# DeltaNet values: from TensorE transposes to VectorE block transposes and a round trip through DRAM

## The chip, the cores and the metric

The kernel runs on one core of one Trainium2 chip. Time is the device time of one execution in microseconds (us), and the median of three executions is given. TensorE (PE in the profile, PEld for its weight loads), VectorE (DVE), ScalarE (ACT), GpSimd (POOL) and SyncE (SP, which issues nearly all DMAs) each work through a queue of their own in order. SBUF is the working memory, PSUM takes the results of TensorE, and what is called a DRAM tensor here is scratch in the chip's main memory.

## The reference

One layer of a hybrid decoder block on a sequence of 1024 tokens with a model width of 2048, all float32:

```
h = rmsnorm(x, ln_g);  proj = h @ w_in
(g_u, g_v, g_z, d_q, d_k, d_v, d_z, d_a, d_b, c_q, c_z) = split(proj)
out_a = gmlp_spatial_gating(g_u, g_v, ...) * silu(g_z)
q, k, v = split(causal_conv_silu(concat([d_q, d_k, d_v]), conv_w))   # 4 taps, 8 heads x 128
o = gated_delta_rule(l2norm(q) * 128**-0.5, l2norm(k), v, g, beta)
out_b = rmsnorm(o, dn_norm_g) * silu(d_z)
out_c = cross_attention(c_q, mem) * silu(c_z)
y = rmsnorm(x + concat([out_a, out_b, out_c]) @ w_out, final_g)
```

In the delta rule of a chunk the values enter as `vb = v * beta`, with one row for each token. The convolution, however, runs along the sequence, so the kernel computes it with channels on the partitions and tokens along the free dimension. Between the two stands a transpose of each head's values, 128 channels x 512 tokens in each half of the sequence.

## The kernel before

**The main stream.** The two large products (`h @ w_in`, `mixed @ w_out`) are done as seven half-size products instead of eight (`seven`, with sums and differences of the halves of both factors). Each of them is a `triple` in a rounded format: the high part times the high part, high times low and low times high. A piece of two weight blocks arrives by DMA in `raw` or `kept`, ACT rounds it to `rhi`, DVE subtracts to get `rlo`; a piece of the left factor goes through `lh` and `ll` (or `lm`) in the same way. There are two buffers of `rhi` and `rlo`. A piece feeds 36 products of 128x512 where a stage has six PSUM banks (`acc` 107 to 110, `dn` 113 and 114), 24 where it has four.

**What runs beside it.** The DeltaNet of eight heads in two halves of the sequence (`hf` 0 and 1) is done in pairs of heads. `front` makes queries and keys and stores them (`late_d`); `inverse` solves 32x32 triangles for four pairs at once in 31 steps on DVE; `levels` joins them to 128x128 blocks on PE; `values` makes the values; `scan_step` runs the recurrence over four tiles of 128 tokens; `heads_out` normalizes the result. `back_of` calls `front_late`, `levels`, `values` and `back` for a pair. Pairs 0 and 1 of both halves run beside the stage of the columns `zv`, pairs 2 and 3 in later stages.

**Values.** For each head `conv` loads 512 tokens (and three before) of the projected values from the DRAM tensor `pd` into `xr`, one of three buffers of 128x515; ACT multiplies the last tap into a tile `tn`, DVE adds the three others, and ACT applies Silu in `tn`. Then `to_tokens` has PE transpose the four 128x128 blocks against `ident` into a PSUM bank that the scan uses too (`dn_111` in the rows below), and `by_token` has ACT copy each block with the token's scale `hs` into the `vs` tile of the pair. Eight pair-halves of two heads make 16 such units and 64 transposes.

**A round trip that is there already.** `turn(tile, src, dst)` transposes on DVE within 32x32 blocks and stores the tile to DRAM; `turned_in(o, src)` loads it back in four DMAs that each put one group of 32 partitions in its place, so that the blocks change places and the whole is transposed. `heads_out` uses it for the scan's output, by the DRAM tensors `od`.

**What sets the order.** Nothing is issued as it is written: `Plan` records every instruction with a cost of its own, computes the dependencies by overlapping regions, lays the work out with a list scheduler in several passes, keeps the best and issues it. A change to one step therefore rebuilds the order of all engines. All instructions carry the line of the issuing loop, L398, so rows are told apart by tile names.

Of the kernel before, what the change touches and what calls it, by code (L numbers as in the profile page):

```python
# [11 lines left out]
AF = mybir.ActivationFunctionType  # L12
# [5 lines left out]
P = 128  # L18
# [4 lines left out]
HT = 512  # L23
# [3 lines left out]
NG, NH, NX = 4, 8, 4  # L27
# [374 lines left out]
def kernel(  # L402
# [29 lines left out]
    V, S, G, PE, Q = R.dve, R.act, R.pool, R.pe, R.sp  # L432
    rank, behind = R.rank, R.behind

    def C(shape, name, dt=F32):
        return sb.tile(list(shape), dt, name=name, tag=name)[:]

    def DT(shape, name, dt=F32):
        return dr.tile(list(shape), dt, name=name, tag=name)[:]
# [41 lines left out]
    def tok(ap):  # L481

        return ap.rearrange("p (t c) -> p t c", c=P)
# [22 lines left out]
    jk = C([P, HT], "jk", mybir.dt.bfloat16)  # L506
# [4 lines left out]
    turn = {"acc": 0, "tp": 0, "dn": 0}  # L511
# [224 lines left out]
    for mt in range(2):  # L736
        t = [ring["ai"](F32R) for _ in range(2)]
# [9 lines left out]
    for h in range(NX):  # L747
        t = ring["vs"](F32R).rearrange("p (s m) -> p s m", s=2)
# [60 lines left out]
    def over(bufs):  # L809
        r = Ring("", 0, None)  # L810
        r.bufs = bufs
        return r
# [38 lines left out]
    r3, ww = ([steps[:, i * P : (i + 1) * P] for i in two] for two in ((0, 1), (2, 3)))  # L851
    scs = [C([P, 12, NT, NH], f"sc{hf}") for hf in range(2)]
    gcs, ecs = ([DT([NT, NH, P], f"{n}{hf}") for hf in range(2)] for n in ("gcd", "ecd"))
    e_d = [[DT([P, NT, P], f"ed{hf}_{h}") for h in range(NH)] for hf in range(2)]
    scan_banks, work = dnr.bufs[0:2], over(dnr.bufs[0:2])
    dnab = over(scan_banks)
# [68 lines left out]
    def to_tokens(*pairs):  # L925
        with R.together():
            for src, tp in pairs:
                for tt in range(NT):
                    PE.transpose(tp[:, tt * P : (tt + 1) * P], src[:, tt * P : (tt + 1) * P], ident)
        return [tok(tp) for src, tp in pairs]  # L930

    def four(t, order):

        return t.rearrange(f"p ({order}) -> p t b i", b=4, t=NT)

    def turn(tile, src, dst):

        V.transpose(four(tile, "b t i"), four(src, "t b i"))
        Q.dma_start(dst, tile)

    def turned_in(o, src):

        v = src.rearrange("(a j) (b n) -> b j a n", a=4, b=4)
        for b in range(4):
            Q.dma_start(o[b * 32 : (b + 1) * 32].rearrange("j (a n) -> j a n", a=4), v[b])

    def conv(which, h, hf, o):
        ct = which * NH + h
        xr = ring["xr"]()
        w = [cw[:, k * 24 + ct : k * 24 + ct + 1] for k in range(4)]  # L950
        if hf == 0:
            G.memset(xr[:, 0:3], 0.0)
            Q.dma_start(xr[:, 3:], p_d[which][h][:, 0:HT])
        else:
            Q.dma_start(xr, p_d[which][h][:, HT - 3 :])
        S.activation(o, xr[:, 3:], AF.Copy, scale=w[3])
        for k in range(3):
            V.scalar_tensor_tensor(o, xr[:, k : k + HT], w[k], o, op0=ALU.mult, op1=ALU.add)
        S.activation(o, o, AF.Silu)

    def by_token(o, src, scale):
        for tt in range(NT):
            S.activation(o[:, tt], src[:, tt], AF.Copy, scale=scale[:, tt : tt + 1])

    def sumsq(o, src):
        for tt in range(NT):
            S.activation(jk[:, 0:P], src[:, tt], AF.Square, accum_out=o[:, tt : tt + 1])

    def qk(h, hf, tiles, hs, gt, bank):

# [2 lines left out]
        beta, edk = (scs[hf][:, i] for i in (0, 4))  # L973
        (kt,) = to_tokens((k, bank))
        sumsq(hs[:, 1], kt)
        V.tensor_scalar(hs[:, 1], hs[:, 1], EPS, None, op0=ALU.add)
        V.reciprocal(hs[:, 3], hs[:, 1])
# [204 lines left out]
    def front(p, hf, banks):  # L1182

        hp = (2 * p, 2 * p + 1)
        gt = ring["gt"]().rearrange("p (h t i) -> p h t i", h=2, i=P)
        for i, h in enumerate(hp):
            tiles, hs = front_sets(), ring["hs"]()
            conv(1, h, hf, tiles[1])
            conv(0, h, hf, tiles[0])
            qk(h, hf, tiles, hs, gt[:, i], banks[i])  # L1190
            V.tensor_copy(late_hs[:, hf, h], hs[:, 0:5:4])
            for d, t in zip(late_d[hf][h], tiles[:4]):
                Q.dma_start(d, t)
        gdr = blocks_out(gt, f"{hf}{p}")
        Q.dma_start(gt_d[hf][p].rearrange("p (h t i) -> p h t i", h=2, i=P), gt)
        return gdr
# [17 lines left out]
    def values(hf, hp, gt, qs, ks, hss, rest, inv):  # L1214
        for i, h in enumerate(hp):
            v = ring["tn"]()
            conv(2, h, hf, v)
            bank = scan_banks[i]
            by_token(rest[i][2], to_tokens((v, bank))[0], hss[i][:, 4])

    def back(hf, hp, gt, qs, ks, hss, rest, inv, ut=None):
        ut = ut or levels(gt, *inv)
# [339 lines left out]
    scan_banks, work = [dnr.bufs[0]] * 2, over(dnr.bufs[0:1])  # L1562
    gdrs = []

    def back_of(p, hf, inv):
        state = front_late(p, hf, inv)
        ut = levels(state[2], *state[-1])
        values(*state)
        back(*state, ut)
# [106 lines left out]
    scan_banks, work = dnr.bufs[0:2], over(dnr.bufs[2:3])  # L1676
# [46 lines left out]
    for n, (tag, to) in enumerate((("gt", mkT), ("inv", mv))):  # L1723
        for i in range(NX // 2):
            t = ring[tag](F32R).rearrange("p (h s m) -> p h s m", h=2, s=2)
# [196 lines left out]
```

## Time and profile before

| what | value |
| --- | --- |
| median of three executions | 1594.31 us (1592.87 to 1595.48) |
| the profiled execution | 1593.81 us, span 1592.1 us |
| granted TensorE clock, mean | 0.997 |
| busy: PE, DVE, ACT, POOL | 1570.2, 1228.7, 963.3, 106.7 us |
| instructions in the span | 24568 |
| moved by DMA | 434.12 MB, 273 GB/s mean |
| value transposes on PE | 64, from 617.1 to 1168.4 us |

The span runs from the first to the last instruction; the device time has 1.7 us more around it. Busy time of PE is the union of overlapping matmuls, so the price of one is read from the distance of starts, not from its duration. In a row of groups the columns are: engine, operation, out<-in, shape and count, then busy us and mean ns of one, then the idle time ahead and what ended it. A number in square brackets in the timeline is idle time just before the row, with its releaser.

### The profile page before, as it was taken

What the parts mean: (1) busy time and instruction counts of PE and PEld (TensorE: products, weight loads), DVE (VectorE), ACT (ScalarE), POOL (GpSimd) and SP (SyncE); (2) the same over time, 40 slices, a digit from 0 to 9 for tenths busy, and PEclk for the clock granted to TensorE, in tenths of its full rate; (3) what the DMA queues carried; (4) which work ended last, traced back from release to release, by engine and by line L of the source; (5) the groups of instructions that cost most, each with busy time, mean ns of one, the idle gap of its engine ahead of it and who ended that gap; (6) DMA issues with size and microseconds to landing.
All of it is one profiled execution on the core that took longest, in us unless ns stands there. A gap on an engine that the chain in (4) does not pass through costs nothing.

```text
span 1592.1 us, 24568 instructions
## 1 busy us (share of the span) xinstructions
PE 1570.2 (99%) x8349; PEld 1315.3 (83%) x8349; DVE 1228.7 (77%) x1818; ACT 963.3 (61%) x2006; POOL 106.7 (7%) x143
## 2 busy tenths in 40 slices
PE   8999999999999999999999989999999999999997
PEld 7988888888887888888888878888888888888886
DVE  6977655877589997777789996867658888688875
ACT  6833255535698436787886557765658864344455
POOL 0100010001000100111111001000000000000001
PEclk9999999999999999999999999999999999999999
DMA  9999966888679898786888988999877989778647
GB/s 320 327 317 346 284 171 183 294 292 245 218 246 315 298 325 254 257 250 205 282 281 277 303 244 245 341 325 309 268 245 253 298 298 347 235 263 293 232 146 276
DMA packets 335951, 434.12 MB, mean 273 GB/s; under 512 B 70089, under 2 KB 160466, under 8 KB 335826
## 3 DMA queue, kind: packets, MB, share of 16 engines
q1 hardware_dynamic: 334098, 429.39, 83.3%
q0 software_dynamic: 1088, 2.10, 0.4%
q8 instruction: 66, 1.08, 0.3%
q10 hardware_dynamic: 640, 1.07, 0.2%
q14 instruction: 59, 0.48, 0.1%
HBM read 332.78 MB, written 99.16 MB: 271 GB/s over the span
## 4 chain that ended last, share of the span: by engine, by line
PE 92%; ACT 3%; DMA 2%; DVE 1%; issue 1%; SPq 0%; POOL 0%; POOLq 0%; ACTq 0%; DVEq 0%
PE acc L398 56%; PE dn L398 35%; ACT jk L398 1%; ACT rhi L398 1%; DMA h0d<-tn 1%; SPq L398 0%; DMA tn<-vd 0%; DMA ut<-in_x_dram 0%; DMA kept<-in_mem_dram 0%; DVE rlo L398 0%; DMA raw<-in_w_in_dram 0%; DVE vs L398 0%; ACT vs L398 0%; DVE tn L398 0%; ACT inv L398 0%
## 5 line engine op out<-in xcount | busy, mean ns | idle before, releaser
L398 PE MATMUL acc<-lh,rhi 128*128 128x512 f32 x1024 | 396.2, 396 | 2.9 <-DVE obs L398 1.2
L398 PE MATMUL acc<-lh,rlo 128*128 128x512 f32 x1024 | 382.9, 397 | 0.0
L398 ACT CAST rhi<-raw 128x1024 fp32r<-128x1024 f32 (+1 forms) x148 | 186.6, 1261 | 248.8 <-PE dn L398 133.8
L398 DVE TENSOR_TENSOR rlo<-raw,rhi 128x1024 fp32r<-128x1024 f32 (+1 forms) x148 | 219.3, 1482 | 109.0 <-ACT rhi L398 98.8
L398 PE MATMUL acc<-ll,rhi 128*128 128x512 f32 x688 | 268.0, 395 | 0.8 <-DVE ll L398 0.8
L398 PEld LDWEIGHTS acc<-lh,rhi 128*128 128x128 f32 x1024 | 192.3, 188 | 41.1 <-issue 1.5
L398 PEld LDWEIGHTS acc<-lh,rlo 128*128 128x128 f32 x1024 | 191.9, 188 | 37.4
L398 DVE TENSOR_TENSOR ll<-ll,lh 128x1024 fp32r<-128x1024 f32 x122 | 148.5, 1217 | 17.3 <-ACT lh L398 17.0
L398 PEld LDWEIGHTS acc<-ll,rhi 128*128 128x128 f32 x688 | 129.6, 189 | 26.4 <-DVE ll L398 1.3
L398 ACT CAST lh<-ll 128x1024 fp32r<-128x1024 f32 x122 | 128.2, 1051 | 29.5 <-PE dn L398 9.0
L398 PE MATMUL acc<-lm,rhi 128*128 128x512 f32 x336 | 130.6, 394 | 0.0
L398 PE MATMUL dn<-lh,rhi 128*128 128x512 f32 x288 | 112.6, 393 | 0.0
L398 PE MATMUL dn<-lh,rlo 128*128 128x512 f32 x288 | 109.7, 393 | 0.0
L398 DVE TENSOR_TENSOR raw<-raw,kept 128x1024 f32<-128x1024 f32 (+1 forms) x56 | 80.9, 1444 | 6.9 <-DMA raw<-in_w_in_dram 5.9
L398 DVE TENSOR_TENSOR rlo<-kept,rhi 128x1024 fp32r<-128x1024 f32 (+1 forms) x29 | 41.8, 1443 | 47.3 <-ACT rhi L398 44.4
L398 PE MATMUL dn<-ll,rhi 128*128 128x512 f32 x192 | 75.2, 393 | 0.0
L398 PEld LDWEIGHTS acc<-lm,rhi 128*128 128x128 f32 x336 | 63.2, 188 | 11.9
L398 ACT CAST rhi<-kept 128x1024 fp32r<-128x1024 f32 (+1 forms) x29 | 35.6, 1229 | 50.3 <-PE dn L398 26.2
L398 PEld LDWEIGHTS dn<-lh,rhi 128*128 128x128 f32 x288 | 54.1, 188 | 10.6
L398 PEld LDWEIGHTS dn<-lh,rlo 128*128 128x128 f32 x288 | 54.0, 188 | 10.5
L398 POOL TENSOR_TENSOR hs<-hs,mhalf 128x4 f32<-128x4 f32 x32 | 48.4, 1515 | 195.3 <-DVE hs L398 194.9
L398 POOL TENSOR_TENSOR small<-small,mhalf 128x1 f32<-128x1 f32 x26 | 21.6, 832 | 562.8 <-DVE small L398 562.8
(421 smaller groups left out, 3449.6 us busy)
## 6 DMA issues: line engine op xcount, KB each, us to landing
raw<-in_w_in_dram SPq DMA_DIRECT2D x120, 512.0 KB
ll<-hsd SPq DMA_DIRECT2D x54, 512.0 KB
raw<-in_w_out_dram SPq DMA_DIRECT2D x48, 512.0 KB
raw<-in_w_in_dram SPq DMA_DIRECT2D x72, 256.0 KB
lm<-hsd SPq DMA_DIRECT2D x26, 512.0 KB
pd<-obs SPq DMA_DIRECT2D x48, 256.0 KB
late<-os SPq DMA_DIRECT2D x44, 256.0 KB
kept<-in_w_in_dram SPq DMA_DIRECT2D x20, 512.0 KB
```

What stands on the lines that cost most here:

```text
L398: o.fn(*o.args, **o.kw)
```

## The change

In `values` the PE transposes and the PSUM bank are dropped. `conv` now returns the first 512 columns of its input buffer `xr`, which it no longer needs. `turn` transposes the values in 32x32 blocks on DVE from `tn` into that buffer and stores it to a new DRAM tensor `vtd` of 256 KB for each head and half. `turned_in` loads the quadrants back into `tn` in four DMAs, and `by_token` reads them from SBUF; a new helper `like` gives source and destination the same shape, since the blocks lie in another order within a row.

```diff
@@ -851,6 +851,7 @@
     r3, ww = ([steps[:, i * P : (i + 1) * P] for i in two] for two in ((0, 1), (2, 3)))
     scs = [C([P, 12, NT, NH], f"sc{hf}") for hf in range(2)]
     gcs, ecs = ([DT([NT, NH, P], f"{n}{hf}") for hf in range(2)] for n in ("gcd", "ecd"))
+    vt_d = [[DT([P, HT], f"vtd{hf}_{h}") for h in range(NH)] for hf in range(2)]
     e_d = [[DT([P, NT, P], f"ed{hf}_{h}") for h in range(NH)] for hf in range(2)]
     scan_banks, work = dnr.bufs[0:2], over(dnr.bufs[0:2])
     dnab = over(scan_banks)
@@ -957,14 +958,19 @@
         for k in range(3):
             V.scalar_tensor_tensor(o, xr[:, k : k + HT], w[k], o, op0=ALU.mult, op1=ALU.add)
         S.activation(o, o, AF.Silu)
+        return xr[:, 0:HT]
 
     def by_token(o, src, scale):
         for tt in range(NT):
-            S.activation(o[:, tt], src[:, tt], AF.Copy, scale=scale[:, tt : tt + 1])
+            S.activation(like(o[:, tt], src), src[:, tt], AF.Copy, scale=scale[:, tt : tt + 1])
 
     def sumsq(o, src):
         for tt in range(NT):
-            S.activation(jk[:, 0:P], src[:, tt], AF.Square, accum_out=o[:, tt : tt + 1])
+            S.activation(like(jk[:, 0:P], src), src[:, tt], AF.Square, accum_out=o[:, tt : tt + 1])
+
+    def like(o, src):
+
+        return o.rearrange("p (b i) -> p b i", b=4) if len(src.shape) == 4 else o
 
     def qk(h, hf, tiles, hs, gt, bank):
 
@@ -1214,9 +1220,10 @@
     def values(hf, hp, gt, qs, ks, hss, rest, inv):
         for i, h in enumerate(hp):
             v = ring["tn"]()
-            conv(2, h, hf, v)
-            bank = scan_banks[i]
-            by_token(rest[i][2], to_tokens((v, bank))[0], hss[i][:, 4])
+            t = conv(2, h, hf, v)
+            turn(t, v, vt_d[hf][h])
+            turned_in(v, vt_d[hf][h])
+            by_token(rest[i][2], four(v, "b t i"), hss[i][:, 4])
 
     def back(hf, hp, gt, qs, ks, hss, rest, inv, ut=None):
         ut = ut or levels(gt, *inv)
```

Rows of the order, of before and of the change apart; numbers after a tile's name tell buffers apart. First the place of pair 0 in the second half, on PE, before the change, with the four transposes of the pair's first head (`dn_111<-ident,tn_86`) among products of the main stream:

```order
L398 MATMUL acc_108<-ll,rhi_77 128x512
L398 MATMUL acc_108<-lh,rlo_75 128x512
L398 MATMUL dn_111<-ident,tn_86 128x128 x4
L398 MATMUL acc_109<-lh,rhi_77 128x512
L398 MATMUL dn_112<-ident,os 128x128 x4
L398 MATMUL acc_109<-ll,rhi_77 128x512
L398 MATMUL acc_109<-lh,rlo_75 128x512
L398 MATMUL acc_109<-lh,rhi_77 128x512
L398 MATMUL acc_109<-ll,rhi_77 128x512
L398 MATMUL acc_109<-lh,rlo_75 128x512
L398 MATMUL acc_110<-lh,rhi_77 128x512
L398 MATMUL acc_110<-ll,rhi_77 128x512
```

Behind these rows stood the second head's transposes and then the scan's first step. With the change, the rows up to that step (`states`, `kT`) on PE are:

```order
L398 MATMUL acc_107<-lh,rlo_74 128x512
L398 MATMUL acc_108<-lh,rhi_76 128x512
L398 MATMUL acc_108<-lm,rhi_76 128x512
L398 MATMUL acc_108<-lh,rlo_74 128x512
L398 MATMUL acc_108<-lh,rhi_76 128x512
L398 MATMUL acc_108<-lm,rhi_76 128x512
L398 MATMUL dn_111<-states,kT_409 128x128
L398 MATMUL dn_111<-states,kT_414 128x128
L398 MATMUL acc_108<-lh,rlo_74 128x512
L398 MATMUL acc_109<-lh,rhi_76 128x512
```

Only products of the main stream stand ahead of the scan's first step now; both groups of value transposes are gone.

The same pair on ACT. Before, from the Silu of the first head (`tn_86<-tn_86`) to the scaled copies out of PSUM (`vs_396<-dn_111`):

```order
L398 ACTIVATE tn_86<-tn_86 128x512
L398 CAST lh<-ll 128x1024
L398 ACTIVATE os<-dn_112,hs_95 128x128 x2
L398 COPY ut_82<-dn_111 64x4x64 x2
L398 ACTIVATE os<-dn_112,hs_95 128x128 x2
L398 ACTIVATE E_84<-E_84,hs_95 128x128 x2
L398 ACTIVATE vs_396<-dn_111,hs_93 128x128 x2
L398 ACTIVATE tn_87<-tn_87 128x512
L398 ACTIVATE vs_396<-dn_111,hs_93 128x128 x2
```

No weight piece was rounded between Silu and copy, and the copies waited for PE. With the change, the Silus of both heads stand on ACT in these rows:

```order
L398 ACTIVATE tn_86<-tn_86 128x512
L398 ACTIVATE jk,hs_95<-dn_112 128x128
L398 ACTIVATE tn_87<-tn_87 128x512
L398 CAST rhi_76<-raw_72 128x1536
L398 CAST lh<-ll 128x1024
```

The rounding of a piece (`rhi_76`) follows the Silus. The first scaled copy (`vs_412<-tn_86`) comes further down on ACT, at the end of these:

```order
L398 CAST rhi_77<-raw_73 128x1536
L398 CAST lh<-ll 128x1024
L398 COPY ym<-dn_114 128x512
L398 ACTIVATE os<-dn_112,hs_95 128x128
L398 COPY y_128<-dn_111 32x256 x2
L398 ACTIVATE os<-dn_112,hs_95 128x128 x3
L398 ACTIVATE E_84<-E_84,hs_95 128x128 x2
L398 ACTIVATE vs_412<-tn_86,hs_93 128x128
```

So the copies moved behind the rounding of two pieces, `rhi_76` and `rhi_77`; they no longer wait for PE but for the loads.

The same pair on SP before, where `od` stores the scan's output of the pair ahead of it and `late` are saved queries and keys:

```order
L398 DMA od_2_261<-kd_394 128x512
L398 DMA gt_478<-gtd_1_256 128x1024
L398 DMA od_3_262<-kd_399 128x512
L398 DMA lm<-hsd_317 128x2x512
L398 DMA xr_90<-pd_4_159 128x515
L398 DMA kd_394<-late_0_2_221 128x512
L398 DMA tblk<-tdra_443 32x8x32
L398 DMA late_6_2_213<-os 128x512
```

The value of the pair had no DMA of its own beside the fills of `xr`. With the change, the SP rows at that place are:

```order
L398 DMA vtd_0_353<-xr_90 128x512
L398 DMA ll<-hsd_317 128x2x512
L398 DMA vtd_1_354<-xr_91 128x512
L398 DMA od_2_261<-kd_410 128x512
L398 DMA od_3_262<-kd_415 128x512
L398 DMA raw_73<-in_w_in_dram 128x2x256
L398 DMA ut_83<-udra_463 32x4x32
L398 DMA tn_86<-vtd_0_353 32x4x128 x4
L398 DMA xr_90<-pd_4_159 128x515
L398 DMA tn_87<-vtd_1_354 32x4x128
L398 DMA xr_92<-pd_4_167 128x515
L398 DMA tn_87<-vtd_1_354 32x4x128 x3
```

Two stores (`vtd`) and eight loads (`tn<-vtd`) are new, the first load seven rows behind its store, and the refills of the convolution's buffers (`xr<-pd`) stand behind or between the loads.

The last place is DVE at the start of the second `inverse` (`sq` and `inv`), before:

```order
L398 COPY lhs<-hs_95 128x8
L398 COPY hs_95<-lhs 128x2x4
L398 COPY lhs<-hs_96 128x8
L398 COPY hs_96<-lhs 128x2x4
L398 TENSOR_TENSOR sq<-inv_488,inv_489 128x31
L398 TENSOR_TENSOR inv_489<-inv_489,sq 128x31
L398 TENSOR_TENSOR sq<-inv_488,inv_489 128x60
L398 TENSOR_TENSOR inv_489<-inv_489,sq 128x30x2
```

Small copies and sums of the fronts stood ahead of the inverse. With the change DVE has there:

```order
L398 TENSOR_TENSOR rlo_74<-raw_72,rhi_76 128x1536
L398 TENSOR_TENSOR ll<-ll,lh 128x1024
L398 STREAM_TRANSPOSE xr_90<-tn_87 128x4x4x32
L398 STREAM_TRANSPOSE xr_91<-tn_88 128x4x4x32
L398 TENSOR_TENSOR sq<-inv_504,inv_505 128x31
L398 COPY hs_93<-lhs 128x2x4
L398 COPY hs_94<-lhs 128x2x4
L398 TENSOR_TENSOR inv_505<-inv_505,sq 128x31
```

Two of the new transposes (`xr<-tn`) stand directly ahead of the first row of the inverse. Three more come between the inverse's end and the end of the gMLP's norm, the other eleven elsewhere.

## The prediction

> **What bounds the kernel now.** I read first the page's engine totals, its 40 slices and its chain of waits, to see which engine carries the end.
>
> ```profile
> PE 1570.2 (99%) x8349; PEld 1315.3 (83%) x8349; DVE 1228.7 (77%) x1818; ACT 963.3 (61%) x2006; POOL 106.7 (7%) x143
> PEclk9999999999999999999999999999999999999999
> PE 92%; ACT 3%; DMA 2%; DVE 1%; issue 1%; SPq 0%; POOL 0%; POOLq 0%; ACTq 0%; DVEq 0%
> ```
>
> TensorE (PE) is busy for 1570.2 of 1592.1 us, at a full granted clock in every slice, and 92% of the chain that ended last is PE itself. So an instruction taken from PE's row shortens the run by its share of that row, unless a wait takes its place; and PE is idle for only 21.9 us in all, so there is little else to win. The next view is the table of stages, for those in which the changed step runs or that lie between.
>
> ```profile
> 617.00:655.00 38.00, 37.92 (x235) 31.83 (x233) 30.20 (x49) 25.34 (x73) 3.35 (x6) 1.00 0.77 235
> 655.00:700.00 45.00, 45.00 (x320) 38.91 (x313) 34.38 (x58) 34.71 (x104) 4.67 (x7) 1.00 0.84 264
> 840.00:880.00 40.00, 40.00 (x187) 33.35 (x186) 37.89 (x69) 22.83 (x50) 5.50 (x6) 1.00 0.84 270
> 880.00:920.00 40.00, 38.76 (x174) 31.94 (x173) 37.07 (x62) 20.45 (x26) 2.45 (x2) 1.00 0.95 296
> 920.00:960.00 40.00, 37.15 (x232) 29.28 (x231) 36.68 (x67) 23.09 (x35) 3.59 (x5) 0.96 0.82 232
> 1000.00:1040.00 40.00, 39.94 (x270) 33.39 (x271) 33.12 (x41) 29.46 (x54) 0.61 (x2) 1.00 0.98 337
> 1040.00:1080.00 40.00, 40.00 (x288) 33.97 (x287) 26.75 (x43) 24.62 (x62) 2.81 (x5) 1.00 0.96 305
> 1120.00:1160.00 40.00, 40.00 (x264) 33.15 (x264) 25.90 (x32) 25.99 (x53) 2.65 (x4) 1.00 0.91 291
> ```
>
> The columns are the stretch and its length, then the busy time of PE, its weight loads, VectorE (DVE), ScalarE (ACT) and GpSimd, the granted clock, the DMA engines' busy share and GB/s. PE is full nearly everywhere. The exception is 880 to 960, where it loses 1.24 and 2.85 us while DVE is busy for 37 of 40 us. The timeline says what ended these waits:
>
> ```profile
> 919.10 0.47 PE L398 MATMUL acc<-lh,rhi 128*128 128x512 f32 x1 [1.25 <-DVE obs L398]
> 928.30 0.49 PE L398 MATMUL dn<-raw,ones 128*128 128x128 f32 x2 [1.65 <-DVE raw L398]
> 929.64 0.77 PE L398 MATMUL acc<-ll,rhi 128*128 128x512 f32 x1 [0.85 <-DVE ll L398]
> ```
>
> All three name DVE, 3.75 us together. That is the one place where PE follows another engine.
>
> **The PE transposes that go.** The tile view gives their number, and a timeline around the first group gives what one group costs the stream.
>
> ```profile
> L398 PE MATMUL dn<-ident,tn x64: 270/272/328, 617.1 to 1168.4; 128*128 128x128 f32 x64
> 616.91 0.39 PE L398 MATMUL dn<-ll,rhi 128*128 128x512 f32 x1
> 617.14 0.60 PE L398 MATMUL dn<-ident,tn 128*128 128x128 f32 x4
> 617.50 0.47 PE L398 MATMUL dn<-lh,rlo 128*128 128x512 f32 x1
> 617.81 0.39 PE L398 MATMUL acc<-lh,rhi 128*128 128x512 f32 x1
> 618.04 0.39 PE L398 MATMUL acc<-ll,rhi 128*128 128x512 f32 x1
> ```
>
> The 272 ns of one transpose overlap with its neighbours, so the price is read from starts. Products start 0.23 us apart (616.91 to 617.14, 617.81 to 618.04). The group of four holds the stream from 617.14 to 617.50, 0.36 us, and the product behind it takes 0.31 instead of 0.23 us until the next one starts, 0.08 more. A group costs 0.44 us; 64 transposes are 16 groups, **7.0 us**. The group's whole price goes, since the products behind it wait for nothing of it.
>
> The Trainium skill, in "VectorE: DVE Perf Modes", section "The three transpose paths", speaks against the change: it gives TensorE 390 ns for a bf16 128x128 block and VectorE 311 ns, VectorE in blocks of 32x32 alone, and its rules for kernel authors advise TensorE for 128x128 where PSUM will do. At the page's 390 ns the estimate for 64 blocks would be 25.0 us gained, so 1569.3 us; this trace has 0.11 us per fp32 block in the stream. The advice weighs the transpose alone; here the rows say that PE is the bound.
>
> **The VectorE transposes that come.** The same operation on the same shape and pattern, and the scaled copies of both kinds, are in the groups by shape; how long DVE waits ahead of such a transpose for ACT is in its waits, and the last row places the second inverse:
>
> ```profile
> L398 DVE STREAM_TRANSPOSE kd<-vs 128x512 f32<-128x512 f32 x16 | 11.3, 704 | 4.5 <-ACT vs L398 4.5
> L398 ACT ACTIVATE vs<-dn,hs 128x128 f32<-128x128 f32 x64 | 18.6, 376 | 5.3 <-PE dn L398 5.1
> L398 ACT ACTIVATE vs<-vs,hs 128x128 f32<-128x128 f32 x64 | 21.0, 395 | 0.7 <-POOL hs L398 0.7
> DVE kd L398 <- ACT vs L398: 4.5, 5, 1.6
> L398 DVE TENSOR_TENSOR sq<-inv,inv x31: 182/351/425, 872.8 to 938.4; 128x31 f32<-128x31 f32 x2, 128x60 f32<-128x60 f32 x2, 128x87 f32<-128x87 f32 x2, 128x112 f32<-128x112 f32 x2
> ```
>
> Sixteen at 704 ns are 11.3 us of DVE between 617 and 1168 us, with waits for the Silu ahead of them like those of kd, 0.9 us mean in 5 of 16. What is queued behind such a wait on DVE are the roundings that PE's products need. In the stretches quoted outside 840 to 960 DVE is idle for 7 to 14 of some 40 us, and that hides them. In the new order two of the sixteen stand directly ahead of the second inverse (shown above on VectorE), whose instructions run from 873 to 938 us; uncovered they cost 2 x 0.70 = 1.4 us, and no more than 0 if they go where the window 840 to 880 shows them: DVE at 37.89 of 40 us with PE at 40.00. I take 0, the row of the window in which they fall, and keep 1.4 for the range.
>
> ACT now reads the values from SBUF instead of PSUM: 395 against 376 ns, 64 x 19 ns = 1.2 us on an engine with 39% to spare; 0 on the path. Its wait for PE ahead of the old copies (5.1 us) goes and is replaced by the landing of the loads.
>
> **The store and the loads.** The kernel already does such a round trip for the scan's output, once per head:
>
> ```profile
> 1215.30 0.70 DVE L398 STREAM_TRANSPOSE kd<-vs 128x512 f32<-128x512 f32 x1
> 1216.03 0.32 SPq L398 DMA_DIRECT2D od<-kd  x1
> 1219.07 2.54 SPq L398 DMA_DIRECT2D ai<-od  x4
> 1228.32 0.73 ACT L398 ACTIVATE kd<-ai,col 128x512 f32<-128x512 f32 x1
> L398 SPq DMA_DIRECT2D ai<-od x32: 302/430/700, 1010.2 to 1221.2; - x32
> L398 SPq DMA_DIRECT2D od<-kd x16: 319/335/430, 653.7 to 1216.0; - x16
> SPq L398 <- DMA od<-kd: 4.0, 4, 2.1
> ```
>
> From the transpose's start to the first reader is 13.0 us, an upper bound, for the reader may have been held by ACT's own order; the store was followed by its loads after 3.04 us. A lower end is 3.77 us, from the transpose's start to the first load's issue. On SyncE's queue (SP) 16 stores at 335 ns and 64 loads at 430 ns are 32.9 us of issuing, spread over 551 us. A load whose store has not landed holds the queue, and what stands behind it are weights, other loads and, new here, the refill of the convolution's buffer. The same situation cost 2.1 us at the worst and 4.0 us in four of the present trips. That is less than the 8.3 us that a weight piece feeds PE (36 products at 0.23 us), so I put it at 0.
>
> Bytes: 16 x (256 KB out + 256 KB back) are 8.4 MB. At the 337 GB/s of the window 1000 to 1040 this is 25 us of transfer inside 551 us. In the fullest stretch, 1000 to 1160, some 4 trips fall, 2.1 MB or 6.2 us, and the windows there leave 2% to 10% of 160 us free, so about 9 us. Tight, but it fits.
>
> The reader's side: in the order of ACT two weight pieces are rounded between the Silu of a pair's first head and the first scaled copy, and the two buffers of rounded weights make ACT wait for PE in between, so at least one piece, 8.3 us, and up to three, 24.9 us, pass there. Against 3.8 to 13.0 us for the trip this covers most, not surely all. If it is late, the scan's first step is late next, and every product behind it in PE's queue. I take 0 lateness, since 13.0 us contains ACT's own delay.
>
> The rest of the order is rebuilt too: the values no longer need the scan's PSUM bank, and the scans stand closer behind the levels. What that does to PE's 21.9 us of idleness has no row; the DVE waits of 3.75 us may go or double, so 3.8 us to both sides.
>
> **Sum.** The profiled execution took 1593.81 us, 1592.1 of them span. 1593.8 - 7.0 + 0 + 0 + 0 = 1586.8. The runs' median is 1594.31, 0.5 above it, so the forecast is **1587.3 us**; with the 3.8 us of the order its own range is 1583.5 to 1591.1. A change under 0.2%, 3.2 us, is about what a measurement of this kernel cannot tell from none; "faster" begins at 1591.1.
>
> **Rivals.** *VectorE gives it back (no change).* Behind 840 us DVE is the engine that PE waits for. If five transposes (two at the inverse, three in the norm that follows) each push PE by 0.70 us plus the 0.9 us wait for the Silu, that is 8.0 us, at 1595.3; with the transposes' own time alone, 3.5 us, it is 1590.8. The middle is 1593.1. For it: the three waits quoted. Against it: 840 to 880, where DVE is as full and PE loses nothing. It decides from 3.8 us of new waits.
>
> *Values come late (slower).* PE's queue is in order, so a scan step whose values are still in flight stops all products. If a pair's trip takes the full 13.0 us against a room of one piece, 8.3, it is 4.7 us late; over 8 pairs 37.6 us, at 1624.9. The gain is gone at 0.88 us per pair (7.0 / 8), and it is slower by over 0.2% from 1.28 us per pair. For it: DMA shares of 0.91 to 0.98 from 1000 us on. Against it: the room is more than one piece for most, and the present trips show only 4.0 us of SP waiting.
>
> *More than the sum.* The 3.75 us behind DVE vanish because the scans move earlier: 1583.5 or less. Only the place of the waits speaks for it.
>
> That PE's transposes would stay in the program is excluded: the new order has none of this kind.
>
> **Chances.** Forecast 0.66, no change by DVE 0.15, late values 0.11, more than the sum 0.08. Faster is 0.66 + 0.08 = 0.74, same 0.15, slower 0.11. The range, 1582 to 1598 us, takes in the better case, the whole DVE rival and late values up to 1.3 us per pair; what is left out is about 1 in 10 above and little below.
>
> **What would show it.** Right: no group dn<-ident,tn, 24 + 16 STREAM_TRANSPOSE on DVE near 700 ns, PE's busy time down by about 7 us, PE's waits still 20 to 25 us, and none of a scan step's matmul (dn<-vs,ut or dn<-steps,ut) longer than a us. The DVE rival: PE's waits behind DVE rlo, ll, obs or raw grow by 4 us or more near the inverse. Late values: ACT's vs<-tn waits for DMA tn<-vtd and PE then sits idle ahead of the scan's first step. The forecast falls if PE's idle time grows by over 3.8 us anywhere in the rebuilt order.

## The result, and the profile after

The changed kernel takes **1589.77 us** (median of 10 executions, 1587.25 to 1592.51) against 1594.10 us (10 executions) for the kernel before on the same chip. The ratio is 0.9973 with a 95% interval of [0.9964, 0.9983], so it is faster by 0.27%, 4.3 us. The forecast was 1587.3 us: the direction is right, 4.3 of the expected 7.0 us arrived, and the time is 2.5 us above the forecast.

The profiled execution of after took 1589.41 us, 1587.4 of them span. The engine totals and the shares of the chain that ended last, from its page:

```profile
PE 1562.1 (98%) x8285; PEld 1307.1 (82%) x8285; DVE 1238.7 (78%) x1834; ACT 969.3 (61%) x2010; POOL 99.9 (6%) x143
PE 86%; DMA 5%; ACT 4%; DVE 3%; issue 1%; SPq 1%; POOL 0%; POOLq 0%; ACTq 0%; DVEq 0%
```

PE's count fell by 64 and its busy time by 8.1 us. Not all of that is the transposes: in the profiled execution of before the granted clock, the share of its full clock that TensorE is given, stands at half for 3.4 us, from 929.7 on (the columns are those of the prediction's table of stages):

```profile
929.70:933.10 3.40, 3.40 (x9) 2.82 (x10) 3.23 (x8) 1.05 (x1) 0.00 (x0) 0.50 0.91 309
934.00:937.00 3.00, 3.00 (x16) 2.48 (x15) 1.37 (x3) 0.98 (x2) 0.00 (x0) 1.00 0.76 278
```

At half the clock 3.4 us do the work of 1.7, so an estimate of 1.7 us of the 8.1 is the clock. Between its start and its end, after's profiled execution has no such stretch. Its idle time rose from 21.9 to 25.3 us (1587.4 - 1562.1), and DMA now has 5% of the chain where it had 2%. That is the shape of the result: the removal arrived, and a part of it came back as waits in which transfers have a share. The groups by shape and the tile view of the new DRAM tensors (count, then minimum, median and maximum ns, first and last start) show the new work at the expected prices:

```profile
L398 DVE STREAM_TRANSPOSE xr<-tn 128x512 f32<-128x512 f32 x16 | 11.2, 704 | 0.8 <-ACT tn L398 0.8
L398 ACT ACTIVATE vs<-tn,hs 128x128 f32<-128x128 f32 x64 | 21.3, 393 | 5.0 <-DVE hs L398 4.3 <-DVE ll L398 0.7
L398 SPq DMA_DIRECT2D tn<-vtd x64: 302/430/1507, 541.6 to 1152.6; - x64
L398 SPq DMA_DIRECT2D vtd<-xr x16: 319/382/803, 515.6 to 1142.2; - x16
```

No wait of the copies `vs<-tn` is ended by a load `tn<-vtd`: what ended them is VectorE. The stages in which PE lost time, with the same columns as in the prediction, show where the idle time moved (the row 960 to 1000 had 39.21 us of PE before):

```profile
655.00:700.00 45.00, 42.17 (x234) 35.80 (x233) 41.70 (x77) 40.63 (x118) 3.75 (x6) 1.00 0.89 282
880.00:920.00 40.00, 39.84 (x178) 32.64 (x178) 38.01 (x68) 21.72 (x31) 2.40 (x3) 1.00 0.97 298
920.00:960.00 40.00, 38.41 (x254) 30.35 (x253) 35.07 (x66) 28.27 (x45) 4.31 (x6) 1.00 0.85 245
960.00:1000.00 40.00, 38.94 (x245) 33.28 (x245) 29.31 (x50) 22.80 (x56) 6.03 (x8) 1.00 0.78 221
1000.00:1040.00 40.00, 38.88 (x244) 32.04 (x243) 30.40 (x40) 29.32 (x59) 0.20 (x1) 1.00 0.98 350
```

From 655 to 700 us PE was full before and now loses 2.83 us of 45; from 1000 to 1040 it lost 0.06 and now 1.12. From 880 to 960 it lost 4.09 before and loses 1.75 now (0.16 and 1.59). The larger waits of PE behind the start of the run, by what ended them (us in total, times, longest):

```profile
PE acc L398 <- DVE ll L398: 1.9, 4, 0.9
PE acc L398 <- ACT lh L398: 1.9, 2, 1.1
PE dn L398 <- DVE states L398: 1.5, 1, 1.5
PE dn L398 <- ACT y L398: 0.8, 1, 0.8
PE acc L398 <- DVE rlo L398: 0.8, 2, 0.5
```

The waits for DVE `raw` (1.65) and `obs` (1.25) that the prediction quoted are gone. Instead PE waits for ACT's `lh` and `y`, and once, 1.5 us long, at a scan step for its `states`.

### The profile page after: what moved, and what is told of

Same layout as the page of the kernel before. It is cut to its first block, busy times and chain, and to the rows that moved or that the text cites. A ratio compares the mean times of both kernels' runs of the same rounds, so it can differ in the third digit from the quotient of the medians.

```text
span 1587.4 us, 24572 instructions
## 1 busy us (share of the span) xinstructions
PE 1562.1 (98%) x8285; PEld 1307.1 (82%) x8285; DVE 1238.7 (78%) x1834; ACT 969.3 (61%) x2010; POOL 99.9 (6%) x143
## 3 DMA queue, kind: packets, MB, share of 16 engines
q1 hardware_dynamic: 345618, 437.78, 85.5%
q0 software_dynamic: 1088, 2.10, 0.4%
## 4 chain that ended last, share of the span: by engine, by line
PE 86%; DMA 5%; ACT 4%; DVE 3%; issue 1%; SPq 1%; POOL 0%; POOLq 0%; ACTq 0%; DVEq 0%
PE acc L398 51%; PE dn L398 34%; DMA raw<-in_w_in_dram 1%; ACT jk L398 1%; ACT rhi L398 1%; SPq L398 1%; DVE rlo L398 1%; DMA h0d<-tn 1%; ACT vs L398 1%; DMA lm<-hsd 0%; DMA ut<-in_x_dram 0%; DVE ll L398 0%; DMA ll<-h0d 0%; DMA vd<-sm 0%; DMA kept<-in_mem_dram 0%
## 5 line engine op out<-in xcount | busy, mean ns | idle before, releaser
L398 PE MATMUL acc<-lh,rhi 128*128 128x512 f32 x1024 | 391.0, 395 | 2.3 <-ACT lh L398 1.9
L398 PE MATMUL acc<-lh,rlo 128*128 128x512 f32 x1024 | 376.3, 395 | 0.8 <-DVE rlo L398 0.8
L398 ACT CAST lh<-ll 128x1024 fp32r<-128x1024 f32 x122 | 128.1, 1050 | 36.6 <-DMA ll<-mixd 9.2
L398 PE MATMUL acc<-rlo,lh 128*128 128x512 f32 x144 | 56.1, 391 | 0.0
```

The source lines that it names most:

```text
L398: o.fn(*o.args, **o.kw)
```

## The experiments

The plan rebuilds the order whenever an instruction changes, which would mix two effects. So in e1 to e4 and e7 to e10 the plan is made with all instructions, and afterwards some are issued as nothing or with other operands (`R.ops` is the plan's list of instructions, `o.fn` what is called to issue one, `o.args` its operands). Every other instruction keeps its place on its engine. Each kernel is compared with the kernel before, run on the same chip in the same series (medians 1594.1 to 1595.9 us). Where kernels of different series are set against each other by their medians, up to 0.7 us of the difference can lie in the chip (1.7 us for e5). Single profiled executions differ by one thing more: e1b, e3, e4, e7, e8 and e9 have one stretch of half clock between start and end, as before has, and after, e2b, e6 and e10 have none. All edits of the changed kernel start from this form of `values`:

```python
t = conv(2, h, hf, v)
n0 = len(R.ops)
turn(t, v, vt_d[hf][h])              # R.ops[n0] on VectorE, R.ops[n0 + 1] the store
turned_in(v, vt_d[hf][h])            # four loads
n1 = len(R.ops)
by_token(rest[i][2], four(v, "b t i"), hss[i][:, 4])   # four copies
```

**e1: the order of before, without PE's transposes.**

```diff
+            n0 = len(R.ops)
+            t = to_tokens((v, bank))[0]
+            n1 = len(R.ops)
+            by_token(rest[i][2], t, hss[i][:, 4])
+            for o in R.ops[n0:n1]:
+                o.fn = lambda *a, **k: None
+            for tt, o in enumerate(R.ops[n1:]):
+                o.args = (o.args[0], tok(v)[:, tt], o.args[2])
```

> The order of the kernel before is kept for every instruction; only the 64 value transposes on TensorE are left out, and ScalarE's scaled copies read the untransposed values from SBUF (so the values are not transposed, which is left out of the computation). It prices the removal alone. All theories: 16 groups x 0.44 us = 7.0 us less, 1594.1 - 7.0 = 1587.1 us. If the removed groups had cover that the row did not show, less than 5 us.

Measured: 1591.93 us, ratio 0.9983 [0.9974, 0.9992], 4.8 us above the expected 1587.1. This run has a fault of its own, which its timeline shows (start, duration, engine, instruction, and in brackets the idle time ahead with what ended it):

```profile
1164.05 0.42 SPq L398 DMA_DIRECT2D tn<-mixd  x1
1168.20 1.43 ACT L398 ACTIVATE vs<-tn,hs 128x128 f32<-128x128 f32 x4 [4.55 <-DMA tn<-mixd]
1170.15 0.50 PE L398 MATMUL acc<-lh,rhi 128*128 128x512 f32 x1 [1.95 <-ACT yu L398]
```

In the order of before, `tn` was free as soon as PE had read it, so its next load stood ahead of the copies. The copies of e1 read `tn` and met a buffer that was being refilled; a 4.55 us wait on ACT became 1.95 us on PE, and a stretch of half clock, e1's second, follows right behind. So e1 doesn't price the removal.

**e1b: the same without that fault.** The copies keep reading the PSUM bank.

```diff
-            for tt, o in enumerate(R.ops[n1:]):
-                o.args = (o.args[0], tok(v)[:, tt], o.args[2])
```

> The kernel before in its own order of instructions, with the 64 transposes of the values on TensorE left out at issue and nothing else: the copies read the same half banks as before, with what an earlier product left there (so the values are wrong numbers; the work and the reads are the same). Unlike e1, no buffer comes free earlier for a copy to meet a refilled one. It prices the removal alone. Removal as the prediction has it (0.44 us a group, 7.0 in all): 1594.1 - 7.0 = 1587.1 us. Rival 'the removal is worth less in this order because the copies are waited for anyway': 1590 to 1592, as e1 gave. Against e4 (1584.6) it tells what the rebuilt order itself is worth: 2.5 us if the removal is worth 7.0, nothing if e1b comes out at 1584.6.

Measured: **1587.35 us** (1586.25 to 1588.14), ratio 0.9955 [0.9943, 0.9968]. That is 6.9 us, against the 7.0 worked out from the distance of starts. The page of its profiled execution (1586.53 us, span 1584.8):

```profile
PE 1563.9 (99%) x8285; PEld 1308.4 (83%) x8285; DVE 1228.3 (78%) x1818; ACT 962.9 (61%) x2006; POOL 105.2 (7%) x143
```

PE's busy time fell by 6.3 us, with one stretch of half clock in both executions, and its idle time went from 21.9 to 20.9: nothing took the place of the transposes. It says what the removal is worth where nothing is added and nothing moves.

**e4: the order of after, without either addition.** The copies read `tn` untransposed.

```diff
+            for o in R.ops[n0:n1]:
+                o.fn = lambda *a, **k: None
```

> The order of the changed kernel is kept; transposes on VectorE, stores and loads are all left out, and the copies read the untransposed values. It differs from the first of these runs in the order alone. 'Order': 1589.8 us, 2.7 us above the first run, with the waits of TensorE in 600 to 720 us still there. 'Trip' or 'VectorE', or both together: 1587.1 us, as the first run, and those waits gone.

Measured: **1584.63 us** (1583.08 to 1586.58), ratio 0.9937 [0.9924, 0.9949]. Against after, with the same order, the two additions cost 5.1 us by the medians and 2.8 us by the profiled executions (1589.41 and 1586.58), or some 4.5 with an estimated 1.7 us taken off e4's, which alone of the two has a stretch of half clock. The theory that the order alone took back the gain would have left 1589.8, and it falls. Against e1b, which has the same work in the order of before, the new order is better by 2.7 us by the medians but equal by the profiled executions (1586.58 and 1586.53), and the intervals of the two ratios overlap. So the order is worth something between 0 and 2.7 us, and not a loss. Its waits moved, though: e4 loses 1.94 us between 655 and 700 us, where e1b loses nothing. The longest of these, 1.5 us for `states`, is the same in after, e2b and e3, so it belongs to the new order.

**e3: the order of after, without VectorE's transposes.** All 80 transfers stay.

```diff
+            R.ops[n0].fn = lambda *a, **k: None
+            o = R.ops[n0 + 1]
+            o.args = (o.args[0], v)
```

> The order of the changed kernel is kept; the 16 new VectorE transposes are left out and the store takes the untransposed values, with all 80 DMAs (the transpose within blocks is left out). 'Order': 1589.8 us, as the changed kernel. 'Trip': 1589.8 us. 'VectorE': the missing 2.7 us come back, 1587.1 us.

Measured: 1587.26 us, ratio 0.9956 [0.9944, 0.9969]: 2.5 us below after, with intervals that just overlap.

**e2 and e2b: the order of after, without the transfers.** In e2 the copies read `xr`, in e2b they read `tn` as in after.

```diff
+            for o in R.ops[n0 + 1 : n1]:
+                o.fn = lambda *a, **k: None
```

e2 had these two lines besides:

```diff
+            for tt, o in enumerate(R.ops[n1:]):
+                o.args = (o.args[0], four(t, "b t i")[:, tt], o.args[2])
```

> The order of the changed kernel is kept; its 16 stores and 64 loads are left out, and ScalarE's copies read the block-transposed tile directly (the exchange of quadrants is left out). Theory 'order' (the missing 2.7 us come from the rebuilt order, in which scan steps stand closer together): no change against the changed kernel, 1589.8 us, ratio 0.997 to before. Rival 'trip' (stores and loads delay values or weights): the full gain comes back, 1587.1 us. Rival 'VectorE' (the new transposes hold back the roundings): 1589.8 us.

> The changed kernel in its own order, with the 80 transfers of the values left out at issue, the 16 VectorE transposes kept; the copies read the buffer of the values as in the changed kernel, where they now find them untransposed (wrong numbers, same work). Unlike e2 the copies don't read the convolution's input buffer, so no load of it overtakes them. Theory 'both additions cost' (e3 and e4: VectorE's part 2.5, the trip's 2.6): 1587.2 us. Rival 'the trip is the whole cost, VectorE's transposes only hurt in company with it': 1584.6. Rival 'the trip costs nothing once a copy isn't delayed by it': 1589.8.

e2 measured 1589.89 us, ratio 0.9972 [0.9963, 0.9981], and has e1's fault in another buffer: the copies waited three times, 8.1 us in all, for the next load of `xr`, which the order of after puts ahead of them. e2b measured **1585.31 us** (1583.32 to 1585.77), ratio 0.9941 [0.9928, 0.9953]. So without the transfers the same kernel is 4.5 us faster by the medians (6.1 by the profiled executions, since e2b's, 1583.32 us, is its fastest), and the 16 transposes on VectorE that it still has cost 0.7 us against e4, which is within the scatter. The two traces show where. ACT rounds the same 177 weight pieces in the same order in all kernels of this order; here are the 89th and the 109th, in after and then in e2b:

```profile
890.78 1.06 ACT L398 CAST rhi<-raw 128x1024 fp32r<-128x1024 f32 x1 [2.94 <-PE acc L398]
1028.55 1.05 ACT L398 CAST rhi<-raw 128x1024 fp32r<-128x1024 f32 x1 [0.98 <-PE acc L398]
```

```profile
890.25 1.06 ACT L398 CAST rhi<-raw 128x1024 fp32r<-128x1024 f32 x1 [3.06 <-PE acc L398]
1022.38 1.05 ACT L398 CAST rhi<-raw 128x1024 fp32r<-128x1024 f32 x1 [0.98 <-PE acc L398]
```

Up to 890 us after is 0.5 us behind e2b, at 1028 it is 6.2 us behind, and so it stays to the last piece (1562.40 and 1556.20). Of the 6.1 us, 5.6 are lost in this one stretch. ACT's waits between 900 and 1050 us that were ended by a transfer (in all, times, longest), the largest, first in after:

```profile
ACT lh L398 <- DMA lm<-hsd: 5.1, 2, 2.9
ACT lh L398 <- DMA ll<-hsd: 4.1, 3, 1.9
ACT rhi L398 <- DMA vd<-sm: 4.0, 1, 4.0
ACT sm L398 <- DMA raw<-in_w_in_dram: 3.0, 1, 3.0
ACT lh L398 <- DMA ll<-h0d: 2.5, 2, 2.3
```

and in e2b:

```profile
ACT lh L398 <- DMA lm<-hsd: 1.9, 1, 1.9
ACT lh L398 <- DMA ll<-hsd: 1.6, 1, 1.6
ACT sm L398 <- DMA vd<-sm: 1.5, 2, 1.2
ACT L398 <- DMA vd<-sm: 1.1, 2, 0.9
```

With the smaller ones they add up to 24.4 us in after and 6.1 in e2b. None of the rows is a transfer of the values: it is mostly the left factor of the main stream (`lm`, `ll`), the gMLP's `vd` and a weight piece that come late. (Outside the stretch one rounding of after waits 6.3 us, at 549.94, and the profile puts it down to `tn<-vtd`; after falls no further behind e2b there.) PE's share in it is the sum row of the four windows from 880 to 1040 us, after and then e2b:

```profile
sum 160.00, PE 156.07 PEld 128.30 DVE 132.79 ACT 102.12 POOL 12.94; mean PE 39.02 PEld 32.08 DVE 33.20 ACT 25.53 POOL 3.24
```

```profile
sum 160.00, PE 159.49 PEld 133.89 DVE 137.62 ACT 104.00 POOL 13.54; mean PE 39.87 PEld 33.47 DVE 34.40 ACT 26.00 POOL 3.38
```

PE idles 3.93 us there in after and 0.51 in e2b; the difference, 3.4 us, is most of the 3.8 us by which their whole idle times differ (25.3 and 21.5). The other 2.3 us of the 6.1 stand in PE's busy time (1562.1 and 1559.8 for the same products), and no row says why. One chain behind PE's idle time, from the timeline of after:

```profile
989.70 0.63 ACT L398 ACTIVATE sm<-sm 128x512 f32<-128x512 f32 x1 [2.96 <-DMA raw<-in_w_in_dram]
990.24 1.85 ACT L398 ACTIVATE vs<-vs,hs 128x128 f32<-128x128 f32 x6
991.99 1.03 ACT L398 CAST lh<-ll 128x1024 fp32r<-128x1024 f32 x1
993.07 1.20 PE L398 MATMUL acc<-lh,rhi 128*128 128x512 f32 x4 [0.76 <-ACT lh L398]
```

ACT stands for 2.96 us behind a transfer, then has a queue of six scaled copies ahead of the next rounding, and PE, which needs that rounding, stops for 0.76 us. In e2b the same instruction starts without a wait:

```profile
983.67 0.62 ACT L398 ACTIVATE sm<-sm 128x512 f32<-128x512 f32 x1
```

**e7: the values never late.** All additions stay, but the copies read a constant.

```diff
+            for tt, o in enumerate(R.ops[n1:]):
+                o.args = (o.args[0], ident.rearrange("p (b i) -> p b i", b=4), o.args[2])
```

> The changed kernel in its own order with all transposes and all 80 transfers, but the 64 copies of the values read a constant tile in place of what the loads bring, so that no copy can wait for the trip (wrong numbers, same work). It parts the trip's cost of some 2.6 us into values that come late and a queue that is busier. If values that come late are the cost: 1587.2 us, as without the trip. If the 80 issues and 8.4 MB on SP's queue are the cost (other loads held up behind them): 1589.8, no change.

Measured: 1589.42 us, ratio 0.9971 [0.9961, 0.9982], the same as after. The time until the values themselves arrive is not the cost. ACT's waits for transfers in the same stretch stay too, 26.4 us; the largest:

```profile
ACT sm L398 <- DMA vd<-sm: 7.5, 4, 3.9
ACT lh L398 <- DMA ll<-hsd: 5.8, 4, 1.9
ACT lh L398 <- DMA lm<-hsd: 5.1, 2, 2.8
```

Yet this execution loses only 2.5 us against e2b from 890 to 1022 us: not every wait of ACT reaches PE. The wait of 2.96 us in the chain above is 2.47 us here, and PE stops for 0.28 us behind it where it stopped for 0.76.

**e8, e9, e10: issues, bytes or the queue.** e8 makes the four loads of a head one plain load; e9 keeps all 80 issues and moves a sixteenth of the rows; e10 lets GpSimd issue them.

```diff
@@ e8
+            o = R.ops[n0 + 2]
+            o.args = (v, vt_d[hf][h])
+            for o in R.ops[n0 + 3 : n1]:
+                o.fn = lambda *a, **k: None
@@ e9
+            o = R.ops[n0 + 1]
+            o.args = (vt_d[hf][h][0:8], o.args[1][0:8])
+            few = vt_d[hf][h][0:8].rearrange("(a j) (b n) -> b j a n", a=4, b=4)
+            for b, o in enumerate(R.ops[n0 + 2 : n1]):
+                o.args = (o.args[0][0:2], few[b])
@@ e10
+            for o in R.ops[n0 + 1 : n1]:
+                o.fn = nc.gpsimd.dma_start
```

> The changed kernel in its own order, but the four loads of a head are one plain load of the whole 128x512 block, in the place of the first (the quadrants aren't exchanged: wrong numbers, same bytes). 48 of the 80 issues of the trip are gone (48 x 430 ns = 20.6 us of SP's time), the 8.4 MB stay. e7 says that values which come late are not the cost, so it is either the issues on SP's queue or the bytes. If the issues: most of the 4.5 us comes back, 1586 to 1587. If the bytes, or the store's own wait: 1589 to 1590.

> The changed kernel in its own order with all 80 transfers of the values issued in their places, but each moves one sixteenth of its rows (8x512 stored, 2x4x128 loaded; the rest of the buffer stays as the convolution left it: wrong numbers, same work on the engines). The counterpart of e8: issues and waits stay, 7.9 of 8.4 MB go. If the issues or the order of SP's queue cost the 4.5 us: 1589 to 1590. If the bytes do: 1585.3, as without the trip.

> The changed kernel in its own order, the 80 transfers of the values issued by GpSimd in place of SP, each at its place in the program; nothing else moves and nothing is left out. SP is free of 33.6 us of issues and of the store's wait for VectorE; GpSimd, which is busy 6% of the span, takes them. If SP's queue is the cost: 1585.3 to 1587, faster than both kernels. If the bytes are: 1589 to 1590. Rival on the slow side: GpSimd's own work (fills and masks of the scan steps) waits behind a store that waits for VectorE, and TensorE behind it: 1591 to 1600.

| kernel | us, median (range) | ratio to before, 95% | ACT's waits for transfers, 900 to 1050 us | lost against e2b, 890 to 1022 us |
| --- | --- | --- | --- | --- |
| after | 1589.77 (1587.25 to 1592.51) | 0.9973 [0.9964, 0.9983] | 24.4 | 5.6 |
| e7, values unread | 1589.42 (1587.60 to 1592.78) | 0.9971 [0.9961, 0.9982] | 26.4 | 2.5 |
| e3, no VectorE transposes | 1587.26 (1584.79 to 1590.50) | 0.9956 [0.9944, 0.9969] | 21.5 | 2.1 |
| e8, one load of four | 1587.39 (1585.18 to 1588.19) | 0.9950 [0.9934, 0.9965] | 7.3 | 1.7 |
| e9, a sixteenth of the bytes | 1586.65 (1584.33 to 1588.92) | 0.9948 [0.9931, 0.9965] | 5.5 | 0.9 |
| e10, GpSimd issues | 1589.54 (1585.36 to 1595.53) | 0.9966 [0.9953, 0.9979] | 10.4 | 1.3 |
| e4, neither addition | 1584.63 (1583.08 to 1586.58) | 0.9937 [0.9924, 0.9949] | 8.4 | 1.2 |
| e2b, no transfers | 1585.31 (1583.32 to 1585.77) | 0.9941 [0.9928, 0.9953] | 6.1 | 0 |

The last two columns are of one execution each. With the whole trip on SP's queue (after, e7, e3) ACT waits 21.5 to 26.4 us for transfers and 2.1 to 5.6 us are lost; without it (e4, e2b) 6.1 to 8.4 and 0 to 1.2. So the side of the difference is shown, and its size in a single execution isn't steady.

e9 has every issue, though shorter ones (263 ns for a load, median, against 430), and 5.2 of the 6.2 us that SP waits for VectorE's `xr` or for the store, and yet most of the 4.5 us is back; so the issues by themselves are not the greater part. e8 has all bytes in a quarter of the loads and in larger packets, and more than half is back; so the bytes by themselves are not either. Both intervals only just touch that of after. What both have less of is packets, by the queue's row of the page (packets, MB, share of 16 engines over the span), in after, e2b, e9 and e8:

```profile
q1 hardware_dynamic: 345618, 437.78, 85.5%
```

```profile
q1 hardware_dynamic: 334098, 429.39, 83.3%
```

```profile
q1 hardware_dynamic: 334994, 429.91, 83.2%
```

```profile
q1 hardware_dynamic: 338706, 437.78, 84.6%
```

The trip is 11520 packets; e9 has 896 of them left and e8 4608. The share tells less, for it scatters: in this order it is 82.7 to 83.3% in the executions without the trip (e2, e2b, e4) and 84.2 to 85.5% in those with all of it (e3, e7, after). That makes the trip 0.9 to 2.8% of 16 engines, 14 to 44 us, in engines that are busy for 0.78 to 0.98 of the four windows from 880 to 1040. This fits transfers that delay one another on the engines. One late load can be followed by its rows, and SP's queue has a part in it: after issues `lm<-hsd` at 909.00 us, behind loads of the values, and ACT rounds it at 914.35 after a wait of 2.92; e2b issues it at 906.85 and e9 at 906.99, and no one waits for it. Less the 0.5 us that after is behind e2b by then, it is issued 1.6 us later. How much of all lateness is the queue's and how much the engines' was not parted. e10 speaks neither for nor against it. By its median nothing is gained, so a free SP queue isn't worth the 4.5 us, but its runs lie 10 us apart, its profiled execution is among the fastest (1586.42 us), so its row of waits is not that of a median run, and why it scatters is open. The rival on its slow side, TensorE behind a GpSimd that waits, would have been 1591 or more; single runs were, the median was not.

**e6 and e5: another order.** One number of the planner, in after (e6) and in before (e5):

```diff
-    SLACK = 300.0
+    SLACK = 400.0
```

> The changed kernel with one number of the planner changed (the allowance ahead of a product that waits for another engine, 300 to 400 ns), which rebuilds the order and leaves all work the same. It asks how far an order drawn anew moves the time. Theory 'an order drawn anew is worth several us either way' (as e4 against the removal suggests): 1584 to 1595, away from 1589.8 by 2 us or more. Rival 'the order is worth little': 1588.8 to 1590.8.

> The kernel before with the planner's allowance ahead of a product raised from 300 to 400 ns, as the changed kernel had it in e6 (1586.3 us); all work is the same, the order is drawn anew. It asks whether e6's gain of 3.4 us on the changed kernel belongs to the allowance or to the one draw. If the larger allowance is better in itself: 1590 to 1592 us. If each order is a draw of its own: anywhere from 1589 to 1599, with no tie to e6. The change in this order is then e6 less this run; the removal's 7.0 less the additions' 0.7 to 5.1 us would leave -2 to -6 us.

e6 measured **1586.34 us** (1585.22 to 1590.14), ratio 0.9956 [0.9941, 0.9971]; e5 1590.53 us (1588.77 to 1594.94), ratio 0.9973 [0.9960, 0.9986]. With the larger allowance before gains 0.27%, with an interval that doesn't reach 1. After gains 0.17%, but the intervals of the two ratios overlap, so that gain isn't shown. With this allowance on both sides the change is worth 0.17% (0.9956 against 0.9973), again with overlapping intervals. e6 is the fastest kernel here that does all the work, 0.44% below before. Its waits are not the same ones: PE waits 1.9 us once for DVE `sq`, the second inverse, which in after it did not:

```profile
PE dn L398 <- DVE sq L398: 1.9, 1, 1.9
```

## Why the prediction was right in direction and short in size

- **PE's transposes, 7.0 us.** Right: 6.9 us in e1b, by the distance of starts (0.36 + 0.08 us a group). The 272 ns a row of the groups gives for one would have made 17.4 us of it.
- **VectorE's transposes, 0 with 1.4 us for the range.** The price (704 ns) is as written; the waits for the Silu, expected to be like those of `kd` (4.5 us), were 0.8 us in all. On the path they cost 0.7 us without the transfers (e2b against e4) and 2.5 us with them (after against e3); the first lies within the scatter, and the intervals of the second just overlap. That VectorE's hold on PE is stronger where ACT, which feeds both, is already late would explain the difference; it was not tested.
- **The round trip, 0: the step that failed.** Its words were "Tight, but it fits". The transfers cost 4.5 us beside VectorE's transposes (after against e2b) and 2.6 without them (e3 against e4). The prediction looked for the cost in three places, a held SP queue, late values and the bytes at 337 GB/s. Late values aren't the cost (e7), and the held queue alone can't be the greater part (e9 keeps most of it), though it has a share. The size of the third, 25 us, lies within the 14 to 44 us of the traces, so the bytes weren't shown to be mis-sized. (The 2% to 10% of the four windows leave 10 us, not 9.) What failed is the reading "it fits": the mean free share of a stretch says nothing of single transfers, and PE waits for single roundings of ACT, which wait for single loads of `ll`, `lm` or `raw`. In after, e7 and e3 ACT's waits for transfers from 900 to 1050 us are 21.5 to 26.4 us, in e2, e2b and e4 4.0 to 8.4. The trace of before gave a warning: 880 to 960 wasn't "the one place where PE follows another engine". In the window 960 to 1000, which the prediction's table leaves out, PE lost 0.79 us, and it waited for a transfer:

```profile
PE dn L398 <- DMA tn<-vd: 0.8, 1, 0.8
```

- **The rebuilt order, 0 within 3.8 us.** It held: 0 to 2.7 us of gain (e4 against e1b). The 1.65 and 1.25 us waits for VectorE went, and in the new order PE loses 1.9 to 2.8 us between 655 and 700 us, where nothing was lost before; that the scans standing closer together cause it fits the wait for `states` but was not tested. The clock wasn't full "in every slice" either: the prediction's own row 920 to 960 has 0.96, and that is the 3.4 us of half clock.
- **The sum.** By medians -6.9 for the removal, -2.7 for the order and +5.1 for the two additions together give -4.5, against -4.3 measured. That they agree proves nothing: after, e4 and e1b each stand in two of the differences and drop out of the sum. What the sum shows is that two errors, an order that was better and additions that were dearer than 0, stood against each other. That the time lies within 2.5 us of the forecast is in part luck.
- **The rivals.** *VectorE gives it back* had the right engine for a part of the cost, but not its mechanism: PE's waits behind `rlo`, `ll`, `obs` and `raw` didn't grow by 4 us near the inverse. *Values come late* didn't happen in after: no copy waited for `tn<-vtd`, and no `dn<-vs,ut` or `dn<-steps,ut` waited over a us; in e6 two did, 2.8 us in all, and it was the faster kernel. *More than the sum* is nearly what the order would have given without the additions: e4 is 1.1 us short of its 1583.5.
- **The signs.** Four were right: the group `dn<-ident,tn` gone, 40 transposes on VectorE near 700 ns, PE's busy time down by about 7 us (8.1, or an estimated 6.4 without the half clock), and the scan's named products without a long wait, though another one, `dn<-states,kT`, waited 1.5 us once. The sign "PE's waits still 20 to 25 us" came out at 25.3, just outside; the growth of 3.4 us, just under the 3.8 set as the limit, is the missing part of the gain.
- **The Trainium skill's rule.** On "VectorE: DVE Perf Modes", section "The three transpose paths": the estimate of 25.0 us from the page's time for one block is refuted by e1b's 6.9. Its advice to stay on TensorE has something in it here, by another way than its table: of the 6.9 us that leaving TensorE brings, 5.1 by the medians (e4) are paid for what VectorE's 32x32 blocks need.

What stays open: whether the trip's cost comes by the number of packets, the bytes in flight or the queue that they hold (e8 and e9 each take away some of several; e10 has fewer packets than e8 and didn't gain), why e10 scatters, and how much of the order's gain is real.

## What to carry to other kernels

When work leaves the engine that bounds a kernel, price the removal by the distance of starts, and price what replaces it by the slack of the resource that it shares, not by its own latency: here the moved values were never late, but they made other transfers late. The stretch where the time went had DMA engines busy for 0.78 to 0.98 of its windows; a mean with some free share is no proof that transfers fit. To part an order rebuilt by a planner from the work itself, keep the order and take the work out at issue; and look first whether a buffer that the change leaves free early isn't refilled under the reader.

## What the runs showed of the hardware

The same 8.4 MB aren't the same number of packets from every queue. Issued by SP the trip took 11520 packets (345618 - 334098). Issued by GpSimd (e10), it is in the other queue's row:

```profile
q0 software_dynamic: 4416, 10.49, 2.0%
```

Against 1088 packets and 0.4% in after that is 3328 packets and 1.6%. Whether that is less work for the engines isn't shown, since the 0.9 to 2.8% from SP's queue lie on both sides of it. The issue takes GpSimd 551 ns for a load, median, where SP has 430, and the median time didn't gain from it.

A wait of PE can cost more than itself. Of the fourteen traces, nine have one or two stretches of 3.4 us at half the granted clock between start and end, ten in all. Each begins within 3 us behind a wait of PE of 1.5 to 2.0 us. Of the fifteen such waits behind the first 150 us, five had no such stretch behind them, among them the 1.5 us for `states` in after and e2b; in e3 and e9 the same wait had one. Against e2b, e9 loses 1.6 us across it. That the wait is what brings the clock down was not tested.
